# The third of the seven gate-and-up products taken as seven products of quartered matrices, interleaved with the fourth

## The chip, the cores and the metric

The kernel runs on one core of a Trainium2 chip. The metric is the device time of one execution in microseconds; three runs of the kernel before took 1035.17, 1035.47 and 1036.06 us. A core has five engines that run side by side and wait for each other by semaphores: TensorE (PE, with its weight loads as PEld), VectorE (DVE), ScalarE (ACT), GpSimd (POOL) and SyncE (SP), which in this kernel issues most DMAs. Each engine works through its instructions in a fixed order, so an instruction that waits holds up those behind it. Matmuls accumulate in PSUM, which has eight banks of 128 x 512 fp32; DVE and ACT read them out into SBUF.

## The reference

One encoder layer on x (1024 tokens, width 1024) in fp32: attention and a pooling mixer, their projection, and a gated feed-forward layer of hidden width 2816, then a norm. The change touches the feed-forward layer:

```python
        x = x + jnp.einsum('bse,ed->bsd', mixed, w_out[layer])
        h2 = rmsnorm(x, norm2_g[layer])
        gate = jnp.einsum('bsd,df->bsf', h2, w_gate[layer])
        up = jnp.einsum('bsd,df->bsf', h2, w_up[layer])
        x = x + jnp.einsum('bsf,fd->bsd', jax.nn.silu(gate) * up, w_down[layer])
    return rmsnorm(x, final_g)
```

## The kernel before

**Precision.** Each fp32 operand is split into a high and a low part: `split` (L119) rounds on ACT (L120) and subtracts on DVE (L121). `mm3` (L159) makes one product of three matmuls, high x high (L161), high x low (L162) and low x high (L163; the names in a row show which two parts meet). Every matmul has a weight load of 128 x 128 of its own.

**Seven products.** Gate and up multiply h2 (1024 tokens x 1024) with 11 groups j of 256 hidden columns of `w_gate` and of `w_up`. Both sides are halved in two directions, and four block products become seven, P1 to P7, in Winograd's form. On the side of h2 stand seven blocks of 512 inputs x 512 tokens, made once ahead of the stage: `b11`, `b21`, `b22` and the sums `t1` to `t4` (`BLOCK`: P1 b11, P2 b21, P6 t2, P7 t3, P5 t1, P3 b22, P4 t4). On the side of the weights stand, per group, two raw tiles `r0` and `r1` that SP loads from `w_gate` and `w_up` (`gu_raw`, L1029) and four sums `s1` to `s4` that POOL makes of them (`gu_sums`, L1063 to L1066). `product` (L1001) runs one of the seven: n = 0 for gate and n = 1 for up, each four chunks of 128 inputs x 3 matmuls of 128x512, 24 matmuls in all. P1, P6, P5 and P3 add up one after another in the same two banks (`c1`), P7 and P4 in two others (`c3`), P2 in `c2`.

**Pages.** The split weights of a product are a page (`gu_page`, L984): high and low, 128x1024 each. Pages are counted, and the count modulo 3 gives the ring of their buffers: `wh`/`wl`, again `wh`/`wl`, and `wr`. A page is so put in the place of the one three before it, and waits until that one's product is done. Pages are made two products ahead. The loop over `todo` runs the products in the order `FIRST` for group 0 and `PRODUCTS` for the others; the page of the last product has number 76, and the last page in `wr` is that of P5 of group 10.

**Features.** After P1, P6 and P5, ACT copies the open sums out of `c1` (`snap`, tiles `sn`). `corner` makes the four quarters of silu(gate) x up: `h11` after P2, `h22` after P5 (P7 in group 0), `h12` after P3, `h21` after P4. In it DVE adds a bank and a copy into `qh` (L1147), ACT takes silu (L1148), DVE adds up's (L1149), POOL multiplies (L1150); `h12` needs no copy (L1144, L1145). `qh` has two buffers. `feature_sum` makes `f1` to `f4` on POOL (L1155; in group 10 on DVE). Seven of these tiles per group go to DRAM (`spill`, DMAs `hsdP`, issued by ACT), and the `h` ring of ten buffers holds them until then.

**Down projection.** The next stage takes the same seven-product form over four sets of groups. Its first products d0 and d1 need the features P1 and P2 of groups 0 and 1, loaded by SP as `r_f0` and `r_f1` into the ring `wr` (`down_load`, L1248), and raw weights `r_wd0`, `r_wd1`; `down_page` splits both. The final gain is loaded over `wmask`, the attention's mask (L1209).

**What sets the order.** The code is written engine by engine in the order that it runs in Python, except that a scheduler places each instruction when it expects its operands. So the order on an engine around the change is that of the built program, and is shown below.

Of the kernel before, what the change touches and what calls it, by code (L numbers as in the profile page):

```python
# [8 lines left out]
F32 = mybir.dt.float32  # L9
# [36 lines left out]
def tile_kernel(  # L46
# [936 lines left out]

    def gu_page(name, src, raw=None):  # L984
        n = count[0]
        count[0] += 1
        hi, lo = page((("wh", "wl"), ("wh", "wl"), ("wr", "wr"))[n % 3], name)
        h2, l2 = (t.rearrange("p (g e) -> p g e", g=2) for t in (hi, lo))
        if raw:
# [79 lines left out]
    a11, a12, a21, a22 = gu_parts(0)  # L1069
    s1, s2 = ([wk_tile("h", 10, f"s{i}_0{n}") for n in range(2)] for i in (1, 2))  # L1070
    operands = {0: dict(P1=a11, P2=a12, P6=s2, P5=s1, P4=a22)}
# [11 lines left out]
    def sum3():  # L1083
        s3 = operands[0]["P7"] = [wk_tile("h", 10, f"s3_0{n}") for n in range(2)]
        for n in range(2):
# [3 lines left out]
    def sum4(n):  # L1089
        s4 = operands[0].setdefault("P3", [])  # L1090
        s4.append(wk_tile("h", 10, f"s4_0{n}"))
        return nc.vector.tensor_tensor(out=s4[n], in0=a12[:, n, :], in1=s2[n], op=ALU.subtract)
# [32 lines left out]
    def snap(j, key, n):  # L1125
        tag = ("h", 10) if (j, key) == (0, "sU4") else ("su" if key == "sU2" else "sp", 2)
        t = snaps[j, key, n] = wk_tile(*tag, f"sn{j}_{key}{n}")
        nc.scalar.activation(out=t, in_=banks["c1", n], func=AF.Copy)
# [4 lines left out]
    def feature(j, name, key):  # L1133
        t = feats[name] = wk_tile("h", 10, f"{name}_{j}")
        if key:
# [3 lines left out]
    def corner(j, name, key, src, to):  # L1139

        h = feature(j, name, to)
        q = wk_tile("q", 2, f"q{name}_{j}")
        if key is None:
            nc.scalar.activation(out=q, in_=banks[src, 0], func=AF.Silu)  # L1144
            nc.vector.tensor_tensor(out=h, in0=banks[src, 1], in1=q, op=ALU.mult)  # L1145
        else:
            nc.vector.tensor_tensor(out=q, in0=banks[src, 0], in1=snaps.pop((j, key, 0)), op=ALU.add)  # L1147
            nc.scalar.activation(out=q, in_=q, func=AF.Silu)  # L1148
            nc.vector.tensor_tensor(out=h, in0=banks[src, 1], in1=snaps.pop((j, key, 1)), op=ALU.add)  # L1149
            nc.gpsimd.tensor_tensor(out=h, in0=h, in1=q, op=ALU.mult)  # L1150

    def feature_sum(j, name, key, a, b, op):
        t = feature(j, name, key)
        eng = nc.gpsimd if j + 1 < NG else nc.vector
        eng.tensor_tensor(out=t, in0=feats[a], in1=feats[b], op=op)  # L1155

    def spill(q=nc.scalar):
# [7 lines left out]
    def after(j, k):  # L1165
# [8 lines left out]
        if k == "P3":  # L1174
            corner(j, "h12", None, "c1", None)
            feature_sum(j, "f1", "P5", "h12", "h22", ALU.add)
            feature_sum(j, "f2", "P6", "f1", "h11", ALU.subtract)
            feature_sum(j, "f3", "P7", "h11", "h12", ALU.subtract)
        if k == "P4":
            corner(j, "h21", "sU2", "c3", "P2")  # L1180
            feature_sum(j, "f4", "P3", "h21", "f2", ALU.subtract)

    todo = [(j, k) for j in range(NG) for k in (PRODUCTS if j else FIRST)]
    for i, (j, k) in enumerate(todo):
        if i + 2 < len(todo):
            j2, k2 = todo[i + 2]
            if (j2, k2) not in pages:
                pages[j2, k2] = gu_page(f"gu{j2}_{k2}", operands[j2][k2])
            if k2 == "P3" and j2 + 1 < NG:
                gu_raw(j2 + 1, 0)  # L1190
            if k2 == "P4" and j2 + 1 < NG:
                gu_raw(j2 + 1, 1)
                operands[j2 + 1] = gu_sums(j2 + 1)
        if i:
            spill()
            if i == 1:
                product(j, k, 0, (0, 1))
                with tc.issue_after(mark["turn", ORDER[-1]].ins):
                    product(j, k, 0, (2, 3))
                    product(j, k, 1)  # L1200
            else:
                for n in range(2):
                    product(j, k, n)
        after(j, k)
        pages.pop((j, k))


    gfb = wmask
    nc.sync.dma_start(out=gfb, in_=final_g.partition_broadcast(P))  # L1209
# [220 lines left out]
```

## Time and profile before

| | |
|---|---|
| time, median of three runs | 1035.47 us |
| profiled execution: span from the first to the last instruction | 1033.6 us |
| TensorE clock granted, mean | 0.998 |
| gate and up, from its first weight load to its last matmul | about 396 to 817 us |

The profiled execution's own time is given by its span alone; the median of the runs stands 1.9 us above it. A row of a timeline gives start, duration, engine, line, operation, the tile written and the tiles read (without buffer numbers: `gu_P` is any product of gate and up, `gu_P_h` and `gu_P_l` the two parts of its page), the shape and, in brackets, how long the engine stood idle before it and what ended that. Matmuls are pipelined: one lasts longer than the distance to the next. The rest of the profile is shown where the prediction uses it.

### The profile page before, as it was taken

Reading aid. Unit: us, or ns where it says so; the run is one execution under the profiler, and the core shown is the slowest. Engines: PE = TensorE matmul, PEld = TensorE weight load, DVE = VectorE, ACT = ScalarE, POOL = GpSimd, SP = SyncE. Lnnn points to the kernel's source line nnn. Section 1 sums busy time; section 2 is a strip of 40 time slices with the busy share of each in tenths; the row PEclk is TensorE's granted clock in tenths of the full one; section 3 lists DMA queues with packets and bytes.
Section 4 is the critical chain, followed back from the end, with each engine's and each line's share of the span. In section 5 each row is a group of like instructions: output and inputs, shape, how many; then the busy total and the mean of one; then the engine's idle time right before and its main releaser. Section 6 shows DMA issues by size and latency. Waiting matters only on the chain.

```text
span 1033.6 us, 14202 instructions
## 1 busy us (share of the span) xinstructions
PE 1024.3 (99%) x5104; PEld 868.9 (84%) x5104; DVE 632.8 (61%) x1000; ACT 454.2 (44%) x733; POOL 381.1 (37%) x312
## 2 busy tenths in 40 slices
PE   9999999999999999999999999999999999999997
PEld 7988888998888888888888888888888888888886
DVE  7565566776886479744433334334334789788886
ACT  7434355665665257533333233233233343333346
POOL 4350121213346043447537536636637510000045
PEclk9999999999999999999999999999999999999999
DMA  7224434333643134343143143143236755353424
GB/s 251 53 47 143 105 81 103 84 102 89 224 175 106 49 136 129 103 143 112 62 132 113 62 133 112 64 131 113 81 113 251 248 204 175 110 198 97 153 92 163
DMA packets 108439, 130.21 MB, mean 126 GB/s; under 512 B 7369, under 2 KB 70353, under 8 KB 108369
## 3 DMA queue, kind: packets, MB, share of 16 engines
q1 hardware_dynamic: 96544, 108.18, 33.4%
q10 hardware_dynamic: 11504, 20.47, 5.2%
q8 instruction: 40, 0.66, 0.2%
q0 software_dynamic: 320, 0.66, 0.2%
q14 instruction: 31, 0.25, 0.1%
HBM read 86.29 MB, written 33.03 MB: 115 GB/s over the span
## 4 chain that ended last, share of the span: by engine, by line
PE 98%; DMA 1%; ACT 0%; DVE 0%; POOL 0%; issue 0%; ACTq 0%; POOLq 0%
PE gu_P L161 14%; PE gu_P L162 14%; PE gu_P L163 14%; PE d L161 7%; PE d L162 7%; PE d L163 7%; PE po L657 4%; PE tp L643 3%; PE o L161 3%; PE o L162 3%; PE qk L161 3%; PE qk L162 3%; PE qk L163 3%; PE o L163 3%; PE v L374 2%; PE z L618 2%
## 5 line engine op out<-in xcount | busy, mean ns | idle before, releaser
L121 DVE TENSOR_TENSOR gu_P_l<-s,gu_P_h 128x1024 fp32r<-128x1024 f32 (+1 forms) x48 | 66.5, 1393 | 98.6 <-ACT gu_P_h L120 98.5
L162 PE MATMUL d<-d,d 128*128 128x512 f32 (+1 forms) x308 | 119.5, 388 | 0.0
L163 PE MATMUL d<-d,d 128*128 128x512 f32 (+1 forms) x308 | 119.5, 388 | 0.0
L629 POOL TENSOR_SCALAR p<-p,rr 128x128 f32<-128x128 f32 (+3 forms) x64 | 48.6, 764 | 175.5 <-DVE rr L628 140.2
L161 PE MATMUL d<-d,d 128*128 128x512 f32 x308 | 107.8, 388 | 0.0
L120 ACT ACTIVATE d<-r_f 128x1536 fp32r<-128x1536 f32 (+1 forms) x28 | 38.8, 1384 | 117.6 <-PE d L162 101.6
L121 DVE TENSOR_TENSOR gu_P_l<-r,gu_P_h 128x1024 fp32r<-128x1024 f32 x32 | 48.9, 1527 | 64.3 <-ACT gu_P_h L120 64.3
L1063 POOL TENSOR_TENSOR s<-r 128x1024 f32<-128x1024 f32 x10 | 24.0, 2401 | 161.9 <-DMA r<-in_w_up_dram 116.0
L120 ACT ACTIVATE gu_P_h<-r 128x1024 fp32r<-128x1024 f32 x32 | 33.8, 1060 | 91.1 <-PE gu_P L162 35.5
L162 PEld LDWEIGHTS d<-d,d 128*128 128x128 f32 x308 | 57.8, 188 | 12.0 <-DVE d L121 0.2
L161 PEld LDWEIGHTS d<-d,d 128*128 128x128 f32 x308 | 57.8, 188 | 12.0
L163 PEld LDWEIGHTS d<-d,d 128*128 128x128 f32 x308 | 57.8, 188 | 11.9
L626 ACT ACTIVATE p<-p,mn 128x128 f32<-128x128 f32 (+3 forms) x64 | 49.3, 772 | 32.8 <-DVE mn L620 29.9
L1291 POOL TENSOR_SCALAR sse<-sse 128x1 f32<-128x1 f32 x7 | 3.5, 494 | 158.1 <-ACT junk L1287 158.1
L1150 POOL TENSOR_TENSOR h<-h,qh 128x512 f32<-128x512 f32 x33 | 44.3, 1345 | 32.3 <-ACT qh L1148 24.1
L648 DVE TENSOR_TENSOR tl<-tp,th 128x512 fp32r<-128x512 f32 (+1 forms) x80 | 49.3, 632 | 10.7 <-ACT th L647 9.7
L120 ACT ACTIVATE gu_P_h<-s 128x1024 fp32r<-128x1024 f32 (+1 forms) x48 | 47.0, 984 | 19.7 <-PE gu_P L162 13.0
L1147 DVE TENSOR_TENSOR qh<-gu_P,sn_sU 128x512 f32<-128x512 f32 x22 | 15.2, 690 | 60.5 <-POOL h L1150 43.2
L121 DVE TENSOR_TENSOR d<-r_f,d 128x1536 fp32r<-128x1536 f32 (+1 forms) x28 | 45.7, 1633 | 10.5 <-ACT d L120 10.5
L163 PE MATMUL qk<-hTh,l_qk 128*128 128x512 f32 x128 | 50.7, 396 | 0.0
L161 PE MATMUL qk<-hTh,h_qk 128*128 128x512 f32 x128 | 50.6, 395 | 0.0
L162 PE MATMUL qk<-hTl,h_qk 128*128 128x512 f32 x128 | 50.4, 394 | 0.0
(337 smaller groups left out, 3067.1 us busy)
## 6 DMA issues: line engine op xcount, KB each, us to landing
r_f<-hsdP SPq DMA_DIRECT2D x77, 256.0 KB
r_wd<-in_w_down_dram SPq DMA_DIRECT2D x22, 512.0 KB
hsdP<-f ACTq DMA_DIRECT2D x43, 256.0 KB
r<-in_w_gate_dram SPq DMA_DIRECT2D x21, 512.0 KB
r<-in_w_up_dram SPq DMA_DIRECT2D x21, 512.0 KB
s<-hi SPq DMA_DIRECT2D x64, 128.0 KB
hsdP<-h ACTq DMA_DIRECT2D x32, 256.0 KB
x<-in_x_dram SPq DMA_DIRECT2D x8, 512.0 KB
```

The source lines that it names most:

```text
L120: mark["hi"] = nc.scalar.activation(out=hi, in_=src, func=AF.Copy)
L121: return eng.tensor_tensor(out=lo, in0=src, in1=f32(hi), op=ALU.subtract)
L161: nc.tensor.matmul(ps, lh, rh, start=start, stop=False, **kw)
L162: nc.tensor.matmul(ps, lh, rl, start=False, stop=False, **kw)
L163: mark["mm"] = nc.tensor.matmul(ps, ll, rh, start=False, stop=stop, **kw)
L626: nc.scalar.activation(out=pr[:, :n], in_=pr[:, :n], func=AF.Exp, scale=-1.0, bias=mn, accum_out=rs)
L629: nc.gpsimd.tensor_scalar(out=pr[:, :n], in0=pr[:, :n], scalar1=rr, scalar2=1.0, op0=ALU.mult, op1=ALU.mult)
L643: nc.tensor.transpose(tp[:, w : w + P], probs[h, 2 * sb + a][:, s * P : (s + 1) * P], ident)
L648: nc.vector.tensor_tensor(out=tl[:, :w], in0=tp[:, :w], in1=f32(th[:, :w]), op=ALU.subtract)
L657: mark["pv"] = nc.tensor.matmul(po[:, first * P : 2 * P], vt[p][:, s, j, :], part[:, o : o + wd], start=(s == 0 and part is th), stop=(s = ...
L1063: g(out=s1, in0=a21, in1=a22, op=ALU.add)
L1150: nc.gpsimd.tensor_tensor(out=h, in0=h, in1=q, op=ALU.mult)
```

## The change

From group 1 on, P3, the product of `b22` with `s4`, is made of seven products Q1 to Q7 of quarters. `b22` is quartered by inputs and tokens, `s4` by gate and up and by inputs. Each Q has two chunks of 128 inputs x 3 matmuls of 128x256: 42 narrow matmuls in the place of 24 wide ones. The quarters' sums of `b22` are made once, behind the first products of group 1 (`fine_steps`: four whole quarters, four subtractions, four splits, three steps behind each product). Those of `s4` are made in place by DVE in each group (`fine_page`, L1214): one subtraction before the first page, three before the second. P3 so has two pages, P3a (Q1, Q2, Q7, Q4; 1024 columns) and P3b (Q5, Q3, Q6; 768 columns), and a group has eight pages.

The results are gathered in the copies that ACT took after P5 (`sU4`): DVE adds each Q out of its bank into a half of gate's or up's copy (`fine_product`, L1249). Q1, Q6, Q5 and Q3 add up in one bank (A), Q7 and Q4 in a second (B), Q2 has a third (C), and each must wait until DVE has read the one before it in its bank.

Products of a group now run in the order P1, P2, P6, P7, P5, P3a, P4, P3b, and the pieces of P3 and P4 are interleaved. To make room, `h` goes from ten buffers to eight, `qh` from two to one, the normed rows move to other tiles, and `wmask` and `junk2` take the quarters' sums; the final gain is loaded when Q5 of group 10 has released `wmask`.

```diff
-        q = wk_tile("q", 2, f"q{name}_{j}")
+        q = wk_tile("q", 1, f"q{name}_{j}")
...
+        t1 = const.tile([P, 2, 2, 256], R, tag="wmask", bufs=1, name=f"fine1_{key}")
+        fine[key, "Q5"] = t1[:, 0, :, :], t1[:, 1, :, :]
...
+        return [
+            whole(*z11), whole(*z12), sub(z11, z12, z11), parts("Q5", z11), whole(*z22), sub(z12, z22, z12),
+            parts("Q7", z12), sub(z22, z22, z11), parts("Q6", z22), whole(*z21), sub(z21, z21, z22),
+            parts("Q4", z21),
+        ]
+
+    def fine_page(j, k, part):
+
+        t = operands[j][k]
+        p0, p1, p2, p3 = (t[:, n, h] for n in range(2) for h in QTR)
...
+        if part == "a":
+            go(p2, p0, p2, ALU.subtract)
+            hi, lo = gu_page(f"gu{j}_{k}a", t)
+            at = dict(Q1=0, Q2=1, Q7=2, Q4=3)
+        else:
+            go(p2, p3, p2, ALU.subtract)
+            go(p1, p1, p2, ALU.subtract)
+            go(p0, p0, p2, ALU.add)
+            hi, lo = gu_page(f"gu{j}_{k}b", t, cols=768)
+            at = dict(Q5=0, Q3=1, Q6=2)
...
+    FINE_BANK = dict(Q1="A", Q6="A", Q5="A", Q3="A", Q7="B", Q4="B", Q2="C")
+    FINE_TO = dict(Q1=(0, 0), Q2=(0, 0), Q7=(1, 1), Q4=(1, 0), Q6=(1, 0), Q5=(1, 1), Q3=(0, 1))
...
+    def fine_product(j, k, q, acc):
...
+        for c in range(2):
+            ws = slice(c * P, (c + 1) * P)
+            mm3(
+                ps, wh[:, ws], wl[:, ws], bh[:, c, :], bl[:, c, :],
+                q in ("Q1", "Q7", "Q2") and c == 0, q in ("Q3", "Q4", "Q2") and c == 1, True,
+            )
+        n, h = FINE_TO[q]
+        out = acc[n][:, QTR[h]]
+        nc.vector.tensor_tensor(out=out, in0=ps, in1=out, op=ALU.add)
...
+        if k == "P3b":
+            acc = [snaps[j, "sU4", n] for n in range(2)]
+            nc.scalar.activation(out=acc[0], in_=acc[0], func=AF.Silu)
+            nc.vector.tensor_tensor(out=acc[1], in0=acc[1], in1=acc[0], op=ALU.mult)
+            feats["h12"] = acc[1]
...
+    LATER = ("P1", "P2", "P6", "P7", "P5", "P3a", "P4", "P3b")
+    todo = [(j, k) for j in range(NG) for k in (LATER if j else FIRST)]
...
+            pieces = dict(
+                P3a=("Q1", "Q2", "Q7", (0, (0, 1)), "Q4"), P4=((0, (2, 3)), "Q6", (1, (0, 1)), "Q5", (1, (2, 3))),
+                P3b=("Q3",),
+            )
...
-    gfb = wmask
+    junk2 = junk_row()
+    gfb = const.tile([P, S], F32, tag="wmask", bufs=1, name="gfb")
```

The built order at the three places that the prediction speaks of follows. In names, `gu6_P1_l` is the low part of the page of P1 of group 6; numbers behind names are buffers.

**A boundary between groups.** DVE, from the splits of group 5's last pages to the first pages of group 6; before:

```order
L121 TENSOR_TENSOR gu5_P4_l_6410<-r1_5_6148,gu5_P4_h_6409 128x1024
L1147 TENSOR_TENSOR qh22_5_6453<-gu5_P70_6383,sn5_sU40_6448 128x512
L121 TENSOR_TENSOR gu6_P1_l_6459<-r0_6_6380,gu6_P1_h_6458 128x1024
L1149 TENSOR_TENSOR h22_5_6452<-gu5_P71_6396,sn5_sU41_6450 128x512
L1147 TENSOR_TENSOR qh21_5_6529<-gu5_P70_6383,sn5_sU20_6372 128x512
L1145 TENSOR_TENSOR h12_5_6487<-gu5_P11_6290,qh12_5_6488 128x512
L121 TENSOR_TENSOR gu6_P2_l_6498<-r0_6_6380,gu6_P2_h_6497 128x1024
L1149 TENSOR_TENSOR h21_5_6528<-gu5_P71_6396,sn5_sU21_6374 128x512
L121 TENSOR_TENSOR gu6_P6_l_6537<-s2_6_6417,gu6_P6_h_6536 128x1024
```

And after (`fineA` and `fineB` are the banks, `sn5_sU4` the copies that gather P3; the rows of L1249 are the adds of Q7, Q4, Q6, Q5 and Q3 in this order):

```order
L1249 TENSOR_TENSOR sn5_sU41_6604<-fineB_5P3_6644,sn5_sU41_6604 128x256
L1154 TENSOR_TENSOR qh21_5_6702<-gu5_P70_6545,sn5_sU20_6533 128x512
L1249 TENSOR_TENSOR sn5_sU41_6604<-fineB_5P3_6644,sn5_sU41_6604 128x256
L1249 TENSOR_TENSOR sn5_sU41_6604<-fineA_5P3_6628,sn5_sU41_6604 128x256
L1156 TENSOR_TENSOR h21_5_6701<-gu5_P71_6558,sn5_sU21_6535 128x512
L121 TENSOR_TENSOR gu6_P1_l_6666<-r0_6_6542,gu6_P1_h_6665 128x1024
L1249 TENSOR_TENSOR sn5_sU41_6604<-fineA_5P3_6628,sn5_sU41_6604 128x256
L121 TENSOR_TENSOR gu6_P2_l_6708<-r0_6_6542,gu6_P2_h_6707 128x1024
L1214 TENSOR_TENSOR s4_6_6622<-s4_6_6622 128x256
L1249 TENSOR_TENSOR sn5_sU40_6602<-fineA_5P3_6628,sn5_sU40_6602 128x256
L121 TENSOR_TENSOR gu6_P6_l_6730<-s2_6_6620,gu6_P6_h_6729 128x1024
L121 TENSOR_TENSOR gu6_P7_l_6768<-s3_6_6621,gu6_P7_h_6767 128x1024
```

`qh21` stood ahead of `h12` and the split of P2's page; now the adds of Q4 and Q6 stand directly behind it, and the split of P1's page, which stood ahead of it, behind them.

**The start of group 1.** PE, from the last matmul of group 0 on; before:

```order
L163 MATMUL gu0_P71_5114<-t4h_4445,gu0_P4_l_4991 128x512
L161 MATMUL gu1_P10_5217<-b11h_4433,gu1_P1_h_5133 128x512
L162 MATMUL gu1_P10_5217<-b11l_4434,gu1_P1_h_5133 128x512
L161 MATMUL gu1_P11_5230<-b11h_4433,gu1_P1_h_5133 128x512
L162 MATMUL gu1_P11_5230<-b11l_4434,gu1_P1_h_5133 128x512
L161 MATMUL gu1_P20_5251<-b21h_4435,gu1_P2_h_5172 128x512
L162 MATMUL gu1_P20_5251<-b21l_4436,gu1_P2_h_5172 128x512
L161 MATMUL gu1_P21_5264<-b21h_4435,gu1_P2_h_5172 128x512
L162 MATMUL gu1_P21_5264<-b21l_4436,gu1_P2_h_5172 128x512
L163 MATMUL gu1_P10_5217<-b11h_4433,gu1_P1_l_5134 128x512
```

And after:

```order
L163 MATMUL gu0_P70_5101<-t4h_4445,gu0_P4_l_4991 128x512
L161 MATMUL gu1_P20_5261<-b21h_4435,gu1_P2_h_5172 128x512
L162 MATMUL gu1_P20_5261<-b21l_4436,gu1_P2_h_5172 128x512
L161 MATMUL gu1_P21_5274<-b21h_4435,gu1_P2_h_5172 128x512
L162 MATMUL gu1_P21_5274<-b21l_4436,gu1_P2_h_5172 128x512
L163 MATMUL gu1_P20_5261<-b21h_4435,gu1_P2_l_5173 128x512
L161 MATMUL gu1_P20_5261<-b21h_4435,gu1_P2_h_5172 128x512
L162 MATMUL gu1_P20_5261<-b21l_4436,gu1_P2_h_5172 128x512
```

Four matmuls each of P1 and P2 with the high parts stood ahead of the first that reads a low part. Now P2 stands ahead of P1 as a whole, and its fifth matmul reads the low part.

**The end of gate and up.** SP's queue around the loads of the first features; before (`hsdP1_0` is feature P1 of group 0; `PE_49` is the semaphore that TensorE raises, here at the end of P5 of group 10):

```order
L1268 DMA x2f_s4_7881<-x2d7_3505 128x1024 [waits DMAHW3_49,DVE_49]
L1268 DMA x2f_r1_7876<-x2d0_3498 128x1024 [waits DMAHW4_49,DMAHW1_49,DVE_49]
L1268 DMA x2f_r1_7876<-x2d1_3499 128x1024 [waits DMAHW5_49]
L1248 DMA r_f0_7843<-hsdP1_0_4819 128x512 [waits DMAHW6_49,PE_49]
L1248 DMA r_f0_7843<-hsdP1_1_4820 128x512 [waits DMAHW7_49]
L1248 DMA r_f1_7849<-hsdP2_0_4830 128x512 [waits DMAHW0_49,PE_49]
L1248 DMA r_f1_7849<-hsdP2_1_4831 128x512 [waits DMAHW1_49]
L1248 DMA r_f7_8107<-hsdP1_2_4821 128x512 [waits DMAHW3_49,DVE_49,Pool_49]
```

And after, where `PE_49` stands for Q5 of group 10 in gfb's row and for Q3 of group 10, the last of gate and up, in those of `r_f0` and `r_f1`:

```order
L1395 DMA x2f_r1_8241<-x2d1_3499 128x1024 [waits DMAHW3_49]
L1395 DMA x2f_s4_8246<-x2d7_3505 128x1024 [waits DMAHW4_49,DVE_49]
L1375 DMA r_f7_8474<-hsdP1_2_4821 128x512 [waits DMAHW6_49,DMAHW0_49,DMAHW7_49,DVE_49,Pool_49]
L1375 DMA r_f7_8474<-hsdP1_3_4822 128x512 [waits DMAHW7_49]
L1375 DMA r_f7_8474<-hsdP1_4_4823 128x512 [waits DMAHW0_49]
L1336 DMA gfb_8203<-in_final_g_dram 128x1024 [waits DMAHW2_49,PE_49]
L1375 DMA r_f0_8208<-hsdP1_0_4819 128x512 [waits DMAHW3_49,PE_49]
L1375 DMA r_f0_8208<-hsdP1_1_4820 128x512 [waits DMAHW4_49]
L1375 DMA r_f1_8214<-hsdP2_0_4830 128x512 [waits DMAHW5_49,PE_49]
```

The loads of `r_f0` and `r_f1` moved behind those of `r_f7` and of the final gain, and wait for the last matmuls of gate and up. On DVE, the same place after the change:

```order
L1249 TENSOR_TENSOR sn10_sU41_8093<-fineB_10P3_8125,sn10_sU41_8093 128x256
L1154 TENSOR_TENSOR qh21_10_8179<-gu10_P70_8037,sn10_sU20_8028 128x512
L1156 TENSOR_TENSOR h21_10_8178<-gu10_P71_8050,sn10_sU21_8030 128x512
L1249 TENSOR_TENSOR sn10_sU41_8093<-fineB_10P3_8125,sn10_sU41_8093 128x256
L121 TENSOR_TENSOR d1_3_8228<-r_wd1_0_8211,d1_2_8227 128x1024
L1249 TENSOR_TENSOR sn10_sU41_8093<-fineA_10P3_8109,sn10_sU41_8093 128x256 x2
L1249 TENSOR_TENSOR sn10_sU40_8091<-fineA_10P3_8109,sn10_sU40_8091 128x256
```

The adds of Q6, Q5 and Q3 (L1249, bank A) stand behind the split of the weights of d1, whose ACT half waits for the last matmul of P4.

More of the change, by code (lines that the diff above doesn't have):

```diff
@@ L1184, in tile_kernel @@
     for i, (j, k) in enumerate(todo):
         if i + 2 < len(todo):
[L1186 to L1193, printed above, removed]
+            next_page(*todo[i + 2])
         if i:
             spill()
[L1196 to L1203, printed above, removed]
+        if i == 1:
+            product(j, k, 0, (0, 1))
+            with tc.issue_after(mark["turn", ORDER[-1]].ins):
+                product(j, k, 0, (2, 3))
+                product(j, k, 1)
+        elif i and (k in ("P3a", "P3b") or k == "P4" and j):
+            acc = [snaps[j, "sU4", n] for n in range(2)]
+            pieces = dict(
+                P3a=("Q1", "Q2", "Q7", (0, (0, 1)), "Q4"), P4=((0, (2, 3)), "Q6", (1, (0, 1)), "Q5", (1, (2, 3))),
+                P3b=("Q3",),
+            )
+            for piece in pieces[k]:
+                if isinstance(piece, str):
+                    fine_product(j, "P3", piece, acc)
+                else:
+                    product(j, "P4", *piece)
+        elif i:
+            for n in range(2):
+                product(j, k, n)
@@ L1204, in tile_kernel @@
         after(j, k)
+        if j == 1 and k == "P1":
+            finer += fine_steps("b22")
+        for _ in range(min(3, len(finer))):
+            finer.pop(0)()
         pages.pop((j, k))
-    gfb = wmask
+    junk2 = junk_row()
+    gfb = const.tile([P, S], F32, tag="wmask", bufs=1, name="gfb")
     nc.sync.dma_start(out=gfb, in_=final_g.partition_broadcast(P))
```

80 lines of the change are left out of this document (68 added, 12 removed).

## The prediction

> **What bounds the kernel now.** The page comes first: busy shares, the granted clock, and the chain that ended last.
>
> ```profile
> span 1033.6 us, 14202 instructions
> PE 1024.3 (99%) x5104; PEld 868.9 (84%) x5104; DVE 632.8 (61%) x1000; ACT 454.2 (44%) x733; POOL 381.1 (37%) x312
> PEclk9999999999999999999999999999999999999999
> PE 98%; DMA 1%; ACT 0%; DVE 0%; POOL 0%; issue 0%; ACTq 0%; POOLq 0%
> PE gu_P L161 14%; PE gu_P L162 14%; PE gu_P L163 14%; PE d L161 7%; PE d L162 7%; PE d L163 7%; PE po L657 4%; PE tp L643 3%; PE o L161 3%; PE o L162 3%; PE qk L161 3%; PE qk L162 3%; PE qk L163 3%; PE o L163 3%; PE v L374 2%; PE z L618 2%
> ```
>
> TensorE is the bound, at full clock, and gate and up (gu_P) hold 42% of the chain. Less TensorE work there shortens the program only if TensorE goes on finding its operands. The windows view of the middle of gate and up shows that it does now, with the other engines far from full:
>
> ```profile
> 420.00:800.00 380.00, 380.00 (x1678) 314.64 (x1677) 155.62 (x150) 132.60 (x175) 207.87 (x112) 1.00 0.35 116
> ```
>
> The columns are PE, PEld, DVE, ACT and POOL, with counts: PE is busy for all of 380 us, 226.5 ns per matmul. So a microsecond of matmul saved is a microsecond gained, and **every new wait of TensorE is a loss in full**.
>
> **The work of TensorE.** Next is PE's timeline: 128x512 matmuls of gate and up, and 128x256 ones of the attention stage, each with a 128x128 load of its own as in the change.
>
> ```profile
> 806.13 0.39 PE L161 MATMUL gu_P<-b22h,gu_P_h 128*128 128x512 f32 x1
> 806.81 0.39 PE L161 MATMUL gu_P<-b22h,gu_P_h 128*128 128x512 f32 x1
> ...
> 175.74 0.28 PE L657 MATMUL po<-th,v 128*128 128x256 f32 x1
> 176.69 0.28 PE L657 MATMUL po<-th,v 128*128 128x256 f32 x1
> ...
> L161 PEld LDWEIGHTS gu_P<-b11h,gu_P_h x88: 187/188/190, 396.0 to 783.5; 128*128 128x128 f32 x88
> ```
>
> Three steps lie between the first two rows: 0.68/3 = 226.6 ns. Eight lie between the next two: 0.95/8 = 119 ns; I take 119.5. A group's third product goes from 24 x 226.6 = 5438 ns to 42 x 119.5 = 5019 ns, 419 ns less. **Ten groups: -4.2 us.** The bound below is half of 226.6 per narrow matmul, -6.8; the nearest rows, at 120, give -4.0.
>
> [...]
>
> **The boundary between groups (nine of them).** The timelines of POOL, DVE, SP and PE around one boundary:
>
> ```profile
> 610.29 0.39 PE L161 MATMUL gu_P<-t1h,gu_P_h 128*128 128x512 f32 x1
> ...
> 612.66 0.37 SPq L1029 DMA_DIRECT2D r<-in_w_gate_dram  x1
> 613.08 0.58 SPq L1029 DMA_DIRECT2D r<-in_w_up_dram  x1
> ...
> 617.99 2.40 POOL L1063 TENSOR_TENSOR s<-r 128x1024 f32<-128x1024 f32 x1 [15.22 <-DMA r<-in_w_up_dram]
> 620.35 2.40 POOL L1065 TENSOR_TENSOR s<-r,r 128x1024 f32<-128x1024 f32 x1
> 622.71 1.29 POOL L1150 TENSOR_TENSOR h<-h,qh 128x512 f32<-128x512 f32 x1
> ...
> 611.41 1.23 DVE L121 TENSOR_TENSOR gu_P_l<-r,gu_P_h 128x1024 fp32r<-128x1024 f32 x1 [4.16 <-ACT gu_P_h L120]
> 624.03 0.69 DVE L1147 TENSOR_TENSOR qh<-gu_P,sn_sU 128x512 f32<-128x512 f32 x1 [5.37 <-POOL h L1150]
> 624.64 0.68 DVE L1145 TENSOR_TENSOR h<-gu_P,qh 128x512 f32<-128x512 f32 x1
> ...
> DVE qh L1147 <- POOL h L1150: 43.2, 8, 5.6
> ```
>
> P5's first matmul starts at 610.29; call that zero. The raw weights of the next group are asked for at +2.4, when the split of P4's page has released their buffer, and land at +7.7. POOL then does s1 and s3, and the product for h22 only at +12.4; DVE stands still until that product is done, at +13.74, and then adds into qh21. The last row, of the waits view, says that this happens in eight groups. Now it is free, since nothing that TensorE needs soon stands behind qh21.
>
> The change leaves these orders as they are and puts something there: behind qh21 on DVE stand the adds of Q4 and Q6 out of PSUM, and Q5 may not start before Q6's bank is read. With qh21 at +13.74, its successor 0.60 later, and two adds of 128x256, Q5 can start at 13.74 + 0.60 + 0.34 + 0.42 + 0.1 = +15.2. The adds' length is that of this row, also an add out of PSUM, the gap between starts shortened as it is for the wide ones (0.60 for 0.68):
>
> ```profile
> L1334 DVE TENSOR_TENSOR x2f_r<-d,x2f_r 128x256 f32<-128x256 f32 x1 | 0.4, 417 | 0.0
> ```
>
> TensorE gets there after P5 (5.44), Q1, Q2 and Q7 (18 x 0.1195 = 2.15), half of P4 (2.72), Q6 (0.72), seven matmuls (1.59), Q4 (0.72) and five (1.13): +14.46. It waits 0.74 us. The pages of P1 and P2 of the next group now wait for Q4 and P4, some 2 us ahead of their use; I add 0.1. **Nine boundaries x 0.85 = +7.6 us.** Bounds: nothing, if the raw weights land 0.8 us sooner; 1.6 each, if P1's split, which now comes behind Q6's add, is also stretched as in the rows of the next part.
>
> [...] If the adds did stretch twofold, 9 x 0.8 = 7 us would come on top. [...] I keep 0.42.
>
> **Start of group 1, once.** DVE's and PE's timelines there:
>
> ```profile
> 434.68 2.48 DVE L121 TENSOR_TENSOR gu_P_l<-r,gu_P_h 128x1024 fp32r<-128x1024 f32 x1 [1.59 <-ACT gu_P_h L120]
> 437.08 0.68 DVE L1147 TENSOR_TENSOR qh<-gu_P,sn_sU 128x512 f32<-128x512 f32 x1
> 437.68 2.82 DVE L121 TENSOR_TENSOR gu_P_l<-r,gu_P_h 128x1024 fp32r<-128x1024 f32 x1
> ...
> 436.21 0.39 PE L161 MATMUL gu_P<-b11h,gu_P_h 128*128 128x512 f32 x1
> 437.11 0.39 PE L161 MATMUL gu_P<-b21h,gu_P_h 128*128 128x512 f32 x1
> ```
>
> Before, four matmuls each of P1 and P2 hide the splits. In the new order P2 comes alone and ahead of P1: four matmuls with the high half, from 436.2 to 437.1, and then the low half, whose split follows P1's at 437.1 and takes 2.8: ready at 439.9, **2.8 us late**. In the same group DVE gets the twelve steps that make the quarters of b22, each 0.7 to 1.3 us, among its splits; I add 0.5 for the page of P7. **+3.3 us**; bounds 0 (the splits at 1.23) and 6.
>
> **End of gate and up, once.** ACT's, SP's and PE's timelines, and the DMA list:
>
> ```profile
> 806.09 19.52 SPq L1248 DMA_DIRECT2D r_f<-hsdP  x13
> ...
> 811.06 1.06 ACT L120 ACTIVATE d<-r_f 128x1024 fp32r<-128x1024 f32 x1 [3.19 <-DMA r_f<-hsdP]
> 817.21 1.07 ACT L120 ACTIVATE d<-r_wd 128x1024 fp32r<-128x1024 f32 x1 [1.09 <-PE gu_P L163]
> ...
> 816.78 0.39 PE L163 MATMUL gu_P<-t4h,gu_P_l 128*128 128x512 f32 x1
> 817.01 0.39 PE L161 MATMUL d<-d,d 128*128 128x512 f32 x1
> ...
> hsdP<-f POOLq DMA_DIRECT2D x1, 256.0 KB, 2.4
> ```
>
> The first features of the down projection (r_f) are asked for at 806.09, eleven microseconds before their matmul at 817.01, which follows on the last one of gate and up without a gap. With one more page per group the last page of gate and up, Q5's, Q3's and Q6's of group 10, lies in the ring whose slots those features reuse, so their load now waits for Q3's last matmuls, the last of all. Three waits follow on each other. (1) Q6's add stands on DVE behind the split of d's second page. Its ACT half starts 0.43 after the last matmul of P4 starts (817.21), then 1.07, 1.23, 0.42 and 0.1: 3.25. TensorE has 0.23 + 0.72 (Q4) to do: it waits 2.3. (2) Q3 waits for Q5's add: 0.28 + 0.42 + 0.1 less one pitch: 0.7. (3) Then the load and its split of 1.06. The row at 806.09 against 811.06 gives 5.0 us from issue to use among other loads, the last row 2.4 for 256 KB alone; with the others done by then but two pieces and the final gain (512 KB) ahead, I take 4.0. With 0.4 of ends and handovers it is 5.5. **Sum +8.5 us**; bounds 6.9 (2.4 for the load) and 11.2 (5.0, and 1.7 for the gain).
>
> **Sum.** -4.2 + 7.6 + 3.3 + 8.5 = +15.2. The span of 1033.6 becomes 1048.8; the 1.9 us by which the median of 1035.47 stands above it stay: **1050.7 us**.
>
> **Rivals.** *The boundaries are covered*: the raw weights land sooner, or POOL takes h22's product first; then 7.6 falls away: 1043. For it, the margin is only 0.74 us; against it, the same 5.4 us wait stands in eight groups, 20%. *Not slower*: the end of gate and up decides alone. With the load at 2.4, d's second split done before P4 ends (so Q5 waits for nothing) and both other places covered, 0.7 + 3.9 stand against -4.2: 1036, and the sign turns when the end costs less than 4.2. Against it, the row at 817.21 waited for P4's last matmul, 6%, a third of it faster. *Narrow matmuls held up by their loads*: at the 188 ns of one load, 42 of them cost 7.90, 2.46 more per group than before: 1050.7 + 4.2 + 24.6 = 1080. [...] Against it, 119 ns between the po rows with the same loads, 3%. *More waits than I count* (bounds of the three places together, 14.4 + 6 + 11.2 - 4.2 = 27): 1057 to 1063, 11%. That the change does not do what it says is excluded: 42 matmuls 256 wide stand in each group's order.
>
> **How the numbers follow.** The forecast has 60% (1045 to 1057). The range of 1040 to 1060 takes in the covered boundaries and most of the dearer case. A measurement here can tell 0.2%, 2.1 us, from no change: faster 4% and same 6%, out of the second rival and the low tails; slower 90%.
>
> **What would show it.** Matmuls 256 wide at 119 to 120 ns; a gap of PE ahead of Q5 put down to DVE in most groups, with qh21 waiting for POOL's h just before; a gap of 2 to 3 us at P2's low half of group 1; and at the end two gaps ahead of Q5 and Q3 and one of 4 to 7 us ahead of the first d matmul, put down to the load of r_f or its split. The prediction fails if PE stays closed at the boundaries, or if the features' load does not end the last wait.

## The result, and the profile after

| | before | after |
|---|---|---|
| time, median of five runs | 1035.77 us | 1058.38 us |
| lowest to highest | 1035.17 to 1036.56 | 1058.12 to 1059.18 |
| ratio, with its 95% interval | | 1.0221 (1.0209 to 1.0233) |
| span of the profiled execution | 1033.6 us | 1056.4 us |

The changed kernel is 22.6 us slower; 15.2 was forecast, and the time lies within the range of 1040 to 1060. The page of the changed kernel, busy shares and granted clock by slices:

```profile
span 1056.4 us, 14666 instructions
PE 1028.6 (97%) x5284; PEld 875.0 (83%) x5284; DVE 696.8 (66%) x1132; ACT 462.8 (44%) x747; POOL 390.8 (37%) x314
PEclk9999999999999999999999999999999899999999
```

TensorE's share falls from 99 to 97%, and for the first time a slice has a lower clock. The waits view of the changed kernel, TensorE's own: who was waited for, the sum, how often, and the longest, in us:

```profile
PE d L161 <- ACT d L120: 4.5, 1, 4.5
PE fineA_10P L161 <- DVE sn_sU L1249: 3.4, 2, 2.9
PE gu_P L163 <- DVE gu_P_l L121: 2.8, 2, 2.3
...
PE fineA_2P L161 <- DVE sn_sU L1249: 1.1, 1, 1.1
...
PE gu_P L161 <- DVE qh L1154: 1.0, 1, 1.0
...
PE fineA_1P L161 <- DVE sn_sU L1249: 0.3, 1, 0.3
```

The rows of `fineA_1P` to `fineA_9P` are Q5 at the nine boundaries (0.3 to 1.1 us; the distance between matmuls grows by a little more), `fineA_10P` is Q5 and Q3 of group 10, `gu_P L163` the low halves of P2 in group 1 and of P1 in group 2, `gu_P L161` the start of P4 of group 10, and `d L161` the first matmul of the down projection. All places of the forecast are there but the page of P7. Where the 22.8 us of span lie is read from PE's timeline: the first P5 matmul of group 0, that of group 10 (`t1h`), and the first of d, after and then before:

```profile
415.09 0.39 PE L161 MATMUL gu_P<-t1h,gu_P_h 128*128 128x512 f32 x1
811.01 0.39 PE L161 MATMUL gu_P<-t1h,gu_P_h 128*128 128x512 f32 x1
837.50 0.80 PE L161 MATMUL d<-d,d 128*128 128x512 f32 x1 [4.46 <-ACT d L120]
```

```profile
414.45 0.39 PE L161 MATMUL gu_P<-t1h,gu_P_h 128*128 128x512 f32 x1
800.69 0.39 PE L161 MATMUL gu_P<-t1h,gu_P_h 128*128 128x512 f32 x1
```

| stretch | before | after | more | forecast |
|---|---|---|---|---|
| start to P5 of group 0 | 414.45 | 415.09 | 0.6 | 0 |
| to P5 of group 10 | 386.24 | 395.92 | 9.7 | 7.1 (-3.8 + 7.6 + 3.3) |
| to the first d matmul | 16.32 | 26.49 | 10.2 | 8.1 (-0.4 + 8.5) |
| to the end of the span | 216.6 | 218.9 | 2.3 | 0 |

**The boundary**, DVE's, POOL's and PE's timelines between groups 5 and 6:

```profile
625.44 2.41 POOL L1070 TENSOR_TENSOR s<-r 128x1024 f32<-128x1024 f32 x1 [12.64 <-DMA r<-in_w_up_dram]
...
630.15 1.31 POOL L1157 TENSOR_TENSOR h<-h,qh 128x512 f32<-128x512 f32 x1
...
631.50 0.69 DVE L1154 TENSOR_TENSOR qh<-gu_P,sn_sU 128x512 f32<-128x512 f32 x1 [5.34 <-POOL h L1157]
632.10 0.41 DVE L1249 TENSOR_TENSOR sn_sU<-fineB_5P,sn_sU 128x256 f32<-128x256 f32 x1
632.55 0.42 DVE L1249 TENSOR_TENSOR sn_sU<-fineA_5P,sn_sU 128x256 f32<-128x256 f32 x1
...
631.55 0.40 PE L163 MATMUL gu_P<-t4h,gu_P_l 128*128 128x512 f32 x1
633.03 0.39 PE L161 MATMUL fineA_5P<-fine_b,gu_P3b_h 128*128 128x256 f32 x1 [1.08 <-DVE sn_sU L1249]
633.25 0.28 PE L162 MATMUL fineA_5P<-fine_b,gu_P3b_h 128*128 128x256 f32 x1
633.73 0.28 PE L163 MATMUL fineA_5P<-fine_b,gu_P3b_l 128*128 128x256 f32 x1
```

DVE stands 5.34 us until POOL has made h22; qh21 and the adds of Q4 and Q6 follow, and Q5 starts 0.06 us behind the second add. Four narrow matmuls take 0.48 us, 120 ns each, but the first one after a wait takes 0.22.

**The end of gate and up**, DVE's, SP's and ACT's timelines (the first row is from group 5, for comparison), and the windows view of PE alone (length, busy time and count, granted clock, DMA share, GB/s):

```profile
615.62 1.22 DVE L1214 TENSOR_TENSOR s<-s 128x256 f32<-128x256 f32 x3
...
809.33 6.49 DVE L1214 TENSOR_TENSOR s<-s 128x256 f32<-128x256 f32 x3
815.74 3.42 DVE L121 TENSOR_TENSOR gu_P_l<-r,gu_P_h 128x1024 fp32r<-128x1024 f32 x1
819.08 0.68 DVE L1154 TENSOR_TENSOR qh<-gu_P,sn_sU 128x512 f32<-128x512 f32 x1
...
827.84 1.66 DVE L121 TENSOR_TENSOR d<-r_wd,d 128x1024 fp32r<-128x1024 f32 x1 [0.38 <-DMA r_f<-hsdP]
829.42 0.41 DVE L1249 TENSOR_TENSOR sn_sU<-fineA_10P,sn_sU 128x256 f32<-128x256 f32 x1
...
832.85 8.13 SPq L1375 DMA_DIRECT2D r_f<-hsdP  x8
...
836.39 1.06 ACT L120 ACTIVATE d<-r_f 128x1024 fp32r<-128x1024 f32 x1 [2.23 <-DMA r_f<-hsdP]
```

```profile
826.70:829.89 3.19, 0.30 (x4) 1.00 0.79 283
829.89:831.39 1.50, 0.98 (x7) 0.92 0.07 25
831.39:832.70 1.31, 1.31 (x6) 0.50 0.55 209
832.70:837.50 4.80, 0.34 (x3) 0.50 0.84 299
837.50:841.40 3.90, 3.90 (x9) 0.50 0.95 322
841.40:851.00 9.60, 9.60 (x43) 1.00 0.99 374
```

The three waits that were forecast follow on each other: Q5's behind the split at 827.84, Q3's, and the load at 832.85, which is split from 836.39 on. Two things were not forecast. DVE is late with P4's page: the three sums of the quarters of s4 ahead of it (809.33) take 6.49 us, against 1.22 in group 5, and its split at 815.74 takes 3.42 in place of 1.23. Behind both stands qh22 (819.08), which reads the bank that P4 needs, so P4 itself starts 1.3 us late. POOL makes sums of its own beside them, 2.6 us each (from 810.41, 812.95 and 815.50), and each of the three quarter sums ends 0.3 us behind the POOL operation in which it began; that they waited for it is the author's reading of these ends, and no run tested it. And 4.2 us after TensorE fell idle, with 1.0 us of work of Q5 in between, its clock drops to 0.50 and stays there until 3.9 us after d's first matmul (831.16 to 841.40): the matmuls of Q3 step at 0.21 us and the first ones of d at 0.43, in place of 0.119 and 0.227.

### The profile page after: what moved, and what is told of

Same layout as the page of the kernel before. It is cut to its first block, busy times and chain, and to the rows that moved or that the text cites. A ratio compares the mean times of both kernels' runs of the same rounds, so it can differ in the third digit from the quotient of the medians.

```text
span 1056.4 us, 14666 instructions
## 1 busy us (share of the span) xinstructions
PE 1028.6 (97%) x5284; PEld 875.0 (83%) x5284; DVE 696.8 (66%) x1132; ACT 462.8 (44%) x747; POOL 390.8 (37%) x314
## 5 line engine op out<-in xcount | busy, mean ns | idle before, releaser
L163 PE MATMUL d<-d,d 128*128 128x512 f32 (+1 forms) x308 | 118.4, 388 | 0.0
L161 PE MATMUL d<-d,d 128*128 128x512 f32 x308 | 109.6, 392 | 4.5 <-ACT d L120 4.5
L161 PEld LDWEIGHTS d<-d,d 128*128 128x128 f32 x308 | 58.5, 190 | 16.9 <-ACT d L120 4.8
L163 PEld LDWEIGHTS d<-d,d 128*128 128x128 f32 x308 | 57.8, 188 | 11.9
L121 DVE TENSOR_TENSOR gu_P_l<-r,gu_P_h 128x1024 fp32r<-128x1024 f32 x32 | 54.4, 1702 | 14.5 <-ACT gu_P_h L120 14.5
L1157 POOL TENSOR_TENSOR h<-h,qh 128x512 f32<-128x512 f32 x33 | 53.8, 1631 | 24.3 <-issue 13.9
L121 DVE TENSOR_TENSOR gu_P_l<-s,gu_P_h 128x1024 fp32r<-128x1024 f32 (+1 forms) x38 | 45.4, 1223 | 21.8 <-ACT gu_P_h L120 21.7
L1154 DVE TENSOR_TENSOR qh<-gu_P,sn_sU 128x512 f32<-128x512 f32 x22 | 15.2, 690 | 54.4 <-POOL h L1157 42.6
L163 PE MATMUL qk<-hTh,l_qk 128*128 128x512 f32 x128 | 50.7, 396 | 0.0
L161 PE MATMUL qk<-hTh,h_qk 128*128 128x512 f32 x128 | 50.6, 395 | 0.0
L1512 DVE TENSOR_TENSOR x2f_s<-d,x2f_s 128x512 f32<-128x512 f32 x64 | 42.7, 685 | 11.5 <-PE d L163 11.4
```

What stands on the lines that cost most here:

```text
L121: return eng.tensor_tensor(out=lo, in0=src, in1=f32(hi), op=ALU.subtract)
L161: nc.tensor.matmul(ps, lh, rh, start=start, stop=False, **kw)
L163: mark["mm"] = nc.tensor.matmul(ps, ll, rh, start=False, stop=stop, **kw)
L1154: nc.vector.tensor_tensor(out=q, in0=banks[src, 0], in1=snaps[j, key, 0], op=ALU.add)
L1512: added = nc.vector.tensor_tensor(out=row, in0=ps, in1=row, op=ALU.add)
```

## Experiments

All times are medians; the kernel before was run beside each on the same chip. Ratios are to it.

**A second buffer for qh.** `e1_second_qh` differs from the changed kernel in one line:

```diff
-        q = wk_tile("q", 1, f"q{name}_{j}")
+        q = wk_tile(*(("sp", 2) if name == "h22" else ("q", 1)), f"q{name}_{j}")
```

> The changed kernel with a second buffer for qh again: qh of h22 takes a slot of the sP1 copies' ring, which is empty at that time. Theory (qh21 stands on DVE until POOL has made h22, because qh has one buffer; the same buffer makes h12 of group 0 late and so puts P2 ahead of P1 in group 1): qh21 no longer waits for POOL's h, the gaps ahead of Q5 in groups 1 to 9 (8.4 us in all) and the P1 page's 0.7 fall to under 1 us together, P1 comes first again in group 1 and its 3.0 us go; the end of gate and up stays. 1058.4 - 8.4 - 0.7 - 3.0 = about 1046.5 us. Rival (Q5 waits because each quarter product in bank A must be read by DVE first, whatever stands on DVE): only group 1's 3.0 us go, the gaps of 0.7 to 1.3 us stay: about 1055.4 us.

Measured: 1059.17 us (ratio 1.0224, 1.0209 to 1.0238), no gain. Its waits view and, for the start of group 2, DVE's, SP's, POOL's and ACT's timelines:

```profile
PE d L161 <- ACT d L120: 5.4, 1, 5.4
PE gu_P L161 <- ACT gu_P_h L120: 5.2, 2, 3.9
...
PE gu_P L161 <- DVE qh L1154: 2.3, 1, 2.3
```

```profile
463.42 1.21 DVE L121 TENSOR_TENSOR gu_P_l<-r,gu_P_h 128x1024 fp32r<-128x1024 f32 x1
...
464.66 0.37 SPq L1036 DMA_DIRECT2D r<-in_w_gate_dram  x1
...
474.75 1.26 POOL L1157 TENSOR_TENSOR h<-h,qh 128x512 f32<-128x512 f32 x1
...
476.04 0.33 ACTq L1254 DMA_DIRECT2D hsdP<-h  x1
476.49 2.00 ACT L120 ACTIVATE gu_P_h<-r 128x1024 fp32r<-128x1024 f32 x2 [6.34 <-POOL h L1157]
```

The mechanism is as expected: no row of Q5 in groups 1 to 9 is left, and group 1 starts with P1 and without a gap. But the next wait was right behind. In group 1 DVE is 4 us late with P4's page (463.42, because it makes the quarters of b22), so the raw weights are asked for late, POOL's h22 is ready at 476.01, and ACT, whose queue holds the DMA of h22 ahead of the split of P1's page, brings P1 4.2 us late; the clock then halves for 3.4 us (0.51 over 477.60 to 481.00, with 8 matmuls; 1.00 over 470.00 to 473.50, with 22). At the end of gate and up P4 starts 2.5 us late instead of 1.3, and the gap ahead of d is 1.0 longer, as the load of the features took 4.5 us from issue to the start of its split (3.5 in the changed kernel). The mean granted clock of the whole execution was 0.989, against 0.994 in the changed kernel, where it stood at a half for 10.2 us between group 1 and d; by an estimate from the two means that is some 10 us more at a half (0.005 x 1057 us x 2). A single cause can be right and its removal worth nothing: the wait moved to the next queue.

**The last group whole, alone and with the buffer.** In `e2_last_group_whole` and `e3_both` the sum for Q4 lies in a quarter of b22, so P3 of group 10 is computed with that sum in the quarter's place. They, and `e7_spill_on_pool` below, leave out putting the quarter back; only their times are used.

```diff
-    todo = [(j, k) for j in range(NG) for k in (LATER if j else FIRST)]
+    todo = [(j, k) for j in range(NG) for k in (FIRST if j == 0 else LATER if j < NG - 1 else PRODUCTS)]
```

> The changed kernel, but group 10 takes P3 whole, as before the change; groups 1 to 9 are as changed. The last page in the ring wr is then again that of P5 of group 10. Theory (the first features' load waits for the last matmuls, three waits follow on each other, and the clock falls while TensorE is idle): from the start of P5 of group 10 to the first d matmul 16.3 us as before in place of 26.5, and the first d matmuls at full clock, 2.3 us more: 1058.4 - 10.2 - 2.3 = about 1045.9 us. Rival (the half clock belongs to the burst of loads at the start of the down projection, not to the idle time): the first d matmuls still step at 0.43 us, about 1048.2 us.

> Both edits together: qh of h22 in the sP1 copies' ring, and P3 of group 10 whole. Theory (all of the loss is in the waits, and the narrow matmuls save 0.3 us per group): 1058.4 - 12.1 - 12.5 = about 1034 us, nine groups at 37.7 to 37.8 us against 38.08 before, so 1 to 2.5 us under the kernel before. Rival (something besides the waits that I listed is dearer, such as the narrow matmuls themselves or the adds): 1036 us or more.

Measured: 1046.93 us (ratio 1.0106, 1.0090 to 1.0122) and 1043.01 us (1.0067, 1.0055 to 1.0078). In `e2_last_group_whole` PE's timeline has P5 of group 10 and d's first matmuls at

```profile
811.73 0.39 PE L161 MATMUL gu_P<-t1h,gu_P_h 128*128 128x512 f32 x1
...
828.05 0.39 PE L161 MATMUL d<-d,d 128*128 128x512 f32 x1
828.28 0.39 PE L162 MATMUL d<-d,d 128*128 128x512 f32 x1
```

16.32 us apart, as before the change to the hundredth, with d at full speed (0.23 us from its first matmul to the next): the theory of the end holds. `e3_both` missed its 1034 by 9 us. PE's timeline shows where: the gap at the start of group 2 is there again (4.2 us, and 1.6 at half clock; the mean granted clock is 0.997, against 0.999 in `e2_last_group_whole`), and its undisturbed groups take 37.9 to 38.4 us, not 37.7.

**The end taken apart.** In `e4_rings_swapped` the pages 85 and 86 change rings; in `e5_d1_on_pool` one split changes engine; `e6_filled` adds matmuls that nothing reads.

```diff
-        hi, lo = page((("wh", "wl"), ("wh", "wl"), ("wr", "wr"))[n % 3], name)
+        hi, lo = page((("wh", "wl"), ("wh", "wl"), ("wr", "wr"))[{85: 2, 86: 1}.get(n, n % 3)], name)
```

> The changed kernel with the rings of the last two pages swapped: the page of P4 of group 10 lies in wr, that of P3b in wh and wl. The features' load then waits for P4's last matmul instead of Q3's, 6 us sooner. Theory (the ring is what holds the load back, and the load what ends the last wait): the load is issued at P4's end, lands in about 5 us and is split by the time Q3 ends; the gap of 4.8 us ahead of the first d matmul shrinks to under 0.7 and the half clock shortens; P4's page comes 0.3 us late. About 1053 us. Rival (the load is held by what is queued ahead of it on SP, or another wait of d takes its place): 1057 us or more, the gap stays above 3 us.

```diff
-        split(wh, wl, moving[b, k])
+        split(wh, wl, moving[b, k], nc.gpsimd if i == 1 else nc.vector)
```

> The changed kernel with one split moved: the low part of the weights of d's second page is made by POOL, not by DVE. Theory (at the end of gate and up Q5 waits for Q6's add, and that stands on DVE behind this split): the gap ahead of Q5 of group 10 falls from 3.1 us to about 1, and all behind it comes 2.1 us sooner: about 1056.3 us, or a little less if the shorter idle time keeps the clock up longer. Rival (Q5 waits for its bank or for qh21 and h21 just the same): the gap stays at 2.5 or more, 1058 us.

```diff
+    def keep_busy(n):
+        for _ in range(n):
+            nc.tensor.matmul(fill[:, 0:256], fh[:, 0, 0:P], fh[:, 0, :], start=True, stop=True)
+
+    keep_busy(16)
+    with tc.issue_after(last):
+        keep_busy(36)
```

> The changed kernel with idle TensorE time filled at the end of gate and up: 16 matmuls of 128x256 ahead of Q5 of group 10 and 36 behind Q3, into a bank that nothing reads; they add work and take no wait away. Theory (the clock falls to a half because TensorE stood idle, some 4 us after the idle time begins, and comes back some 4 us after work resumes): the granted clock stays at 1.0 through the end of gate and up, Q3 and the first d matmuls step at 0.12 and 0.227 us, and the kernel is 2.3 to 3 us faster for doing more: about 1055.7 us. Rival (the half clock comes with the burst of loads of 300 GB/s and more): the first d matmuls still step at 0.43 us, and the time stays at 1058.4 us or above.

| run | time, us | ratio (interval) | what its trace shows |
|---|---|---|---|
| e4_rings_swapped | 1056.13 | 1.0190 (1.0173 to 1.0208) | no gap ahead of d; P4 2.1 us late |
| e5_d1_on_pool | 1057.15 | 1.0206 (1.0189 to 1.0223) | Q5's gap 1.1 us, d's gap 6.3 |
| e6_filled | 1058.31 | 1.0224 (1.0208 to 1.0240) | full clock at the end; d starts 1.0 us later |

`e4` confirms the ring: with the load asked for at P4's end the gap ahead of d is gone. It was worth 2.3 us, not the 5.4 expected, because P4's page in wr came 2.1 us late (0.3 was expected) and the clock dropped behind P4's start (0.50 over 823.10 to 825.30) and again ahead of Q5 (0.50 over 833.00 to 834.30 and 834.40 to 838.00). In the profiled execution it also dropped in group 1 (0.83 over 437.50 to 441.00), where `e4` changes nothing. The four executions differ: the two with a mean granted clock of 0.996 and 0.997 took 1055.15 and 1053.64 us, those with 0.991 and 0.992 took 1057.11 and 1057.72. `e5` confirms that Q5 waited for Q6's add behind d's split (3.1 to 1.1 us), but brought 1.2 us instead of 2.1: d started at 836.1 in place of 837.5, the gap ahead of it 1.6 us longer, since the load of the features took 5.1 us from issue to the start of its split, against 3.5, and from d's first matmul to the end of the span it took 219.8 us (1055.9 less 836.1), against 218.9. The intervals of `e5` and of the changed kernel (1.0209 to 1.0233) overlap, so a gain as small as this is not sure. `e6` settles the clock at the end of gate and up; PE's windows there:

```profile
832.00:834.00 2.00, 2.00 (x19) 1.00 0.93 242
834.00:838.00 4.00, 2.93 (x25) 1.00 0.98 328
838.00:842.00 4.00, 3.50 (x15) 1.00 0.81 300
```

With TensorE kept busy the clock stays at 1.00 under the same loads of 300 GB/s, so the half clock follows the idle time, not the loads; in the last window of the changed kernel, above, the clock is at 1.00 with 374 GB/s. The time did not fall with it: from d's first matmul to the end it took 217.4 us (1055.9 less 838.50) in place of 218.9, but d started 1.0 us later. The load of the features was asked for 0.3 us sooner (832.52) and took 4.9 us to the start of its split: between 3.5 and 5.1 us in `e1`, `e5`, `e6` and the changed kernel, it varies by more than there was to win. Why it does was not tried.

**The next wait, and a mended kernel.** `e7_spill_on_pool` is `e3_both` with the DMA of h22 issued by POOL:

```diff
-            q.dma_start(out=d, in_=h)
+            (nc.gpsimd if key == "P4" else q).dma_start(out=d, in_=h)
```

> The kernel of both edits (qh of h22 in the sP1 copies' ring, P3 of group 10 whole) with one DMA moved: h22's tile is sent to DRAM by POOL, which makes it, and not by ACT. Theory (with the wait on DVE gone the next one stands on ACT: the DMA of h22 waits in ACT's queue for POOL's product, and the split of P1's page of the next group is behind it; at the start of group 2, where the raw weights come 4 us late because DVE was busy with the quarters of b22, this costs 4.2 us, and 1.6 more at half clock): the gap of 4.2 us at the start of group 2 and the half clock behind it go, as do the gaps of 0.4 to 0.9 us ahead of P1 in groups 5 and 6: 1043.0 - 4.2 - 1.6 - 1.6 = about 1035.6 us. Rival (P1's page waits for its raw weights or its ring, not for ACT's queue): the gap stays, 1042 us or more. As in the runs with P3 of group 10 whole, one quarter of b22 then holds the sum for Q4, so the last group's h12 is made with that in its place.

Measured: 1037.55 us (ratio 1.0015, 1.0006 to 1.0024). The gap at the start of group 2 is gone, as the waits view of that run shows: what TensorE still waits for in gate and up is 0.3 us once and 0.2 once.

```profile
PE gu_P L163 <- DVE gu_P_l L121: 0.3, 1, 0.3
```

`e8_all_mended` makes group 1 whole too and puts b22's quarter back ahead of group 10, so that nothing is left out. Beside the lines above:

```diff
+    todo = [(j, k) for j in range(NG) for k in (FIRST if j == 0 else LATER if 1 < j < NG - 1 else PRODUCTS)]
...
+        return [
+            add(y, *fine["b22", "Q5"]), add(z, *fine["b22", "Q1"]),
+            lambda: nc.vector.tensor_tensor(out=z, in0=y, in1=z, op=ALU.add),
+            lambda: split(quarter(bh, 0, 1), quarter(bl, 0, 1), z),
+        ]
```

> All waits found so far mended, with the reference's output: qh of h22 in the sP1 copies' ring, h22 sent to DRAM by POOL, group 1 whole as well (the quarters of b22 are then made two steps behind each of its products), group 10 whole, with the quarter of b22 that Q4's sum had replaced put back ahead of it by three adds and a split. Eight groups take the narrow products. Theory (the narrow products are worth 0.3 to 0.35 us a group once nothing waits): 1035.5 - 8 x 0.35 + 0.3 to 0.4 per group for the restarts around them, that is between 1032.7 and 1035.9 us. Rival (the interleaved order costs by itself): above 1036.5 us.

Measured: 1040.60 us (1.0037, 1.0024 to 1.0051), with one wait left, in the waits view:

```profile
PE d L161 <- ACT d L120: 3.2, 1, 3.2
```

With two pages fewer the last page in wr is that of P3, one product later than P5: the ring again, unintended. Two ways to set it right, `e9_ring_again` by a swap in group 10 and `e10_count_from_one` by the count's start:

```diff
-(("wh", "wl"), ("wh", "wl"), ("wr", "wr"))[n % 3]
+(("wh", "wl"), ("wh", "wl"), ("wr", "wr"))[{82: 2, 83: 1}.get(n, n % 3)]
```

> The mended kernel with the rings of two pages of group 10 swapped: with group 1 whole there are two pages fewer, so the last page in wr is that of P3, not of P5, and the features' load comes 5.4 us later. With P5's page in wr and P3's in wh and wl, theory (the count of pages alone decides when the features can be loaded): the 3.6 us ahead of the first d matmul and the 1.9 us at half clock behind it go, 1040.6 - 3.4 - 1.9 = about 1035.3 us, eight groups at 38.0 us on the mean, within 0.2% of the kernel before. Rival (the load waits for something that the putting back of b22's quarter makes late): the gap stays above 2 us, 1039 us or more.

```diff
-    count = [0]
+    count = [1]
```

> The mended kernel with every page one place further in the rings (the count starts at one): the last page in wr is again that of P5 of group 10, and no page of that group is made later than its neighbours. Theory (the ring's last page decides when the features can be loaded; the other swap only moved a wait to P5's page): no gap above 0.5 us from group 1 to the down projection, d's first matmul directly behind P4's last, 1040.6 - 3.4 - 1.9 = about 1035.3 us, eight groups at 38.0 us on the mean, within 0.2% of the kernel before. Rival (something else in the mended kernel holds d or the last group up): 1038 us or more.

`e9` took 1040.18 us (1.0041, 1.0028 to 1.0055): the gap ahead of d went as expected, but P5's low half came 2.3 us late (its page in wr, and DVE's split of 3.4 us beside POOL's sums and behind the putting back of b22), and the clock dropped again (0.90 over 800 to 805, 0.76 over 805 to 810). `e10` took 1037.75 us (1.0018, 1.0009 to 1.0027), and in its timeline d follows on P4 without a gap:

```profile
817.02 0.39 PE L163 MATMUL gu_P<-t4h,gu_P_l 128*128 128x512 f32 x1
817.25 0.39 PE L161 MATMUL d<-d,d 128*128 128x512 f32 x1
```

From P5 of group 1 to P5 of group 10 it takes 342.4 us (458.56 to 800.93), before 342.7 (457.97 to 800.69). So with every wait of a few tenths or more removed, eight groups of narrow products gain 0.35 us in all. The span is 1.2 us longer than before's all the same: 0.6 more lies ahead of group 1, and 0.9 behind d's first matmul. The 0.6 is no more than executions differ by: P5 of group 0 starts between 414.29 and 415.46 us in the traces of the ten experiments, none of which aims at anything ahead of it. What lengthens the down projection stays open. No version tried beats the kernel before.

## Why the prediction was right, point by point

**Direction and range: right.** The waits that it named, but that of P7's page, are in the trace, each at its place, and the runs that took one away showed the cause it gave. The size was short: 22.8 us of span against 15.2. The time lies above the 1045 to 1057 that had 60%, where *more waits than I count* stood with 11%, but not by the three places reaching their bounds. Of the 7.6 us missing, 1.6 belong to the boundaries; the clock (2.3), wide matmuls that step more slowly (1.3) and P4's late start (1.3) were in no bound. That the range had room for them is luck.

**The work of TensorE, -4.2: right for the narrow matmuls; the wide ones were put at no change.** In PE's timeline 41 of the 42 narrow matmuls of a group step at 119.1 ns on the mean, as the po rows did, so the 0.42 us a group is there. The first matmul of Q5, behind its wait, steps at 0.22; with it the 42 take 5.11 us, and that tenth is counted here with the gaps at the boundary. What was missing: the wide matmuls, above all those of P4 and P1, among which the narrow ones now run, step more slowly (a wide one behind a wide one at 228.0 to 231.5 ns on the mean in these two, by which parts meet, in place of 226.6). From P5 of group 0 to P5 of group 10 this takes back 1.3 us of the 3.9 that the narrow ones save. Why the wide ones step more slowly stays open. In `e10`, where the waits view has no wait of TensorE left between 420 us and d, 0.04 of 0.43 us a group are left (342.7 less 342.4, over eight groups); where the rest went is not shown.

**The boundary, +7.6: right.** The gaps ahead of Q5 in groups 1 to 9 add up to 8.5 us with their restarts, and P1's low half waits 0.7 once, 9.2 in all; the page of P1, for which 0.1 stood at each boundary, waited this once only. The adds out of PSUM kept to what was put in: all 70 took 0.41 to 0.43 us, also the 40 that ran wholly beside a POOL operation, so the 7 us of adds stretched twofold did not come. `e1` showed the reason for the gaps. That P2 stood ahead of P1 in group 1 had the same reason, which the prediction did not see: the single buffer of qh.

**Group 1, +3.3: right** (3.0 in PE's timeline: 2.5 at P2's low half, 0.3 at P6, the rest restarts). The wait of P7's page, 0.5, did not come. The forecast did not follow the quarters of b22 on DVE any further; in `e1` they cost 4.2 us at the start of group 2.

**The end, +8.5: mechanism right, mis-sized.** Q5 (3.05 against 2.3), Q3 (0.7) and the load (4.8 against 5.5) were as forecast, 8.5 in sum. Missing was P4's own start, 1.3 us late. The forecast looked for no wait there: beside POOL's sums the change's three quarter sums took 6.49 us in place of 1.22 and the split of P4's page 3.42 in place of 1.23. It had used such longer operations at group 1 only.

**Not in the sum at all: the clock.** "TensorE is the bound, at full clock" was carried over into a kernel that stops. Half a microsecond in Q3 and 1.8 in d come from it: nine steps from d's first matmul on take 3.97 us in place of 2.15 (an estimate: 0.34 for the first, as behind the wait at 440.26 in group 1, and eight of 0.227). `e6` ties it to the idle time, and in `e2`, where d follows without a wait, the time from d's first matmul to the end is 216.6 us, as before. The 0.6 us ahead of P5 of group 0, where the code is the same, lies within what executions differ by there.

The rivals: "the boundaries are covered" and "not slower" fell with the gaps seen. "Narrow matmuls held up by their loads" fell with 119 ns, 0.53 of the 226.6 of a wide one.

## What to carry to other kernels

Saved matmul time of 0.4 us per group is less than nearly every wait that the new operations brought (0.3 to 1.1 us at a boundary), so follow each new operation into the queue where it will stand, and ask what stands ahead of it and for whom that waits; and when one wait goes, look for the next one behind it before counting the gain. Count what a buffer ring holds last: a few pages more or fewer moved the first load of the next stage by several microseconds, in both directions. When TensorE has stopped for two or three microseconds, it can pay again afterwards, in clock, as here behind 2.4 us in group 1 of `e4` (0.83 and 0.73 granted, in the windows below). An operation that is short in one place can be five times as long in another, beside another engine's work (here 6.49 us against 1.22 for the three quarter sums), so read its length at the place where the wait would be.

## What the runs showed of the hardware

The clock of TensorE fell to 0.50 some 2 to 4 us after an idle time began (2.1 in group 1 of `e4`, 4.2 at the end of the changed kernel) and came back 3 to 4 us after work resumed (3.1 and 3.9 there). By the trace's own record of the clock it stayed down for 10.24 us at the end of the changed kernel (831.16 to 841.40); in group 1 of `e4` it was some 3.4 us, an estimate from the first two windows below: (0.17 x 3.50 + 0.27 x 4.00) x 2. The length of the idle time alone does not decide: in group 1 of `e4` the clock fell 2.1 us into an idle time of 2.4 us; in the changed kernel it did not fall at the same place, with the same code, in 2.3 us, nor in the 2.9 us ahead of Q5 of group 10 (1.00 over 826.70 to 829.89). What else decides was not shown. PE's windows of `e4` and then of the changed kernel:

```profile
437.50:441.00 3.50, 1.09 (x3) 0.83 0.01 2
441.00:445.00 4.00, 4.00 (x14) 0.73 0.17 66
```

```profile
437.50:441.00 3.50, 1.16 (x5) 1.00 0.01 2
441.00:445.00 4.00, 4.00 (x19) 1.00 0.17 66
```
